# Sample scores of four batches side by side on TensorE, and the sample's rows spread over four partitions each, in a hybrid decoder step

## The chip, the core and the metric

The kernel runs on one core of a Trainium2 chip. The metric is the time of one execution on the device in microseconds; lower is better. TensorE multiplies matrices, VectorE and ScalarE work on tiles element by element, GpSimd does some of that and issues the gathers, SyncE issues the other DMAs. Each engine carries out its own instructions in order and waits for others by semaphores.

## The reference

One layer of a decoder is computed for a prompt of 512 rows and for a sample group of 8 batches with 4 new rows each (32 rows), width 1024. Cut to what matters here:

```python
mods = (silu(c) @ w_ada + b_ada)            # six rows of 1024 for the prompt and for each sample batch
h = rmsnorm(x, g_norm1) * (1 + mods[1]) + mods[0]
q, k, v, gates, z, xbc, dt = split(h @ w_in)
# sample attention, per batch of 4 rows: compressed blocks, 15 selected blocks of 64, a window of 512
s = q @ keys.T * SCALE ; p = masked_softmax(s) ; o = p @ values
att = g0 * o_cmp + g1 * o_sel + g2 * o_win   # 8 query heads on 2 key heads of 64
y_ssm = ssd_mixer(...)
mixed = concat([rmsnorm(att, g_att_out), y_ssm]) @ w_out
x = x + mods[2] * mixed
h = rmsnorm(x, g_norm2) * (1 + mods[4]) + mods[3]
y = x + mods[5] * hier_moe(h)                # top 1 of 4 groups, top 2 of 4 experts, 16 experts
```

Prompt and sample go through the same layer with the same weights; the sample reads its older keys and values from paged caches.

## The kernel before, in words

The program is one long function, `hybrid_step`. A framework schedules it: the code says what depends on what, and a list scheduler with its own estimate of durations lays every engine's instructions in a fixed order. `tc.high_priority(offset)` and `tc.add_manual_dep` (an order between two instructions) influence it; `in_turn` ties TensorE's instructions of some helpers to the order in which they are written. So a changed instruction can move others on every engine.

Four stages follow one another. First come the modulation rows and the input projection. The rows of modulation that are needed late are computed by `ada_block` (L290 on) into the tile `mods`, 128 partitions by 8 by 128: partition 32 j + r holds, for row r of nine (the prompt and eight batches), the j-th quarter of 512 columns. The tile is stored to DRAM as `modd` (L760) and read back from there as rows.

Second comes the attention. `attend(t, br)` computes the prompt's attention of row tile t (128 rows, eight heads): two products into PSUM (`s`), a maximum (L815), an exponential (L817), transpositions (L820) and value products (`ot`). Between them the sample's parts are laid. For half hb (four batches) and half h of a batch's past, `gather_half` (L1047) gathers 128 partitions x 8 rows per batch; `sel_part` works on them in two chunks `c4`. In a chunk, `transposed` (L1020 to L1026) turns one batch's keys, four 128x128 blocks into one PSUM bank of the tag `sm` (two buffers), and `evac` (L100 on VectorE, L102 on ScalarE) copies them to a tile `kt` (five buffers). Then one product per batch b4 writes that batch's scores to partitions 32 b4 to 32 b4 + 31 of the bank `smo`, behind a product with `Eb` that writes the mask. `win_half` does the same for the window without a mask. Two halves, two halves of the past, two chunks and two windows make ten groups of four scores. After the softmax the weights are turned and multiplied with the values (`weighted`).

Third come the out-projection and the router. The joined rows are turned and split into a high and a low part (`catH`, `catL`); the weight is split likewise (`wh` and `wl` for the first 512 columns, `wH` and `wL` for the last 512, L1692 and L1693). The sample's part of the product (`samp_k`) lies in PSUM with column quarter j on partitions 32 j to 32 j + 31, and `samp_out` copies the quarters side by side into 32 rows of 1024. Then the sample's residual (L1699, L1700), its normalised row `h2` (`sample_rows`, L1655 to L1668), the router's logits and `rank` follow in 32 partitions. `OSEQ` names the order in which prompt tiles (`m`, `f`, `r`) and the sample (`s`) are written. At the end the tokens are counted per expert and the first rows are gathered.

Fourth, 16 experts and one extra tile are worked off, three products each, with weights loaded ahead by SyncE. Weights of the first expert are issued between the constants of the out-projection.

The helper `mm` records every product under L92, and the copies of `evac` stand under L100 and L102.

## Time and profile before

| What | Value |
|---|---|
| median of 3 runs | 784.91 us (782.52 to 787.93) |
| the profiled execution | 787.62 us |
| its span, first to last instruction | 785.9 us |
| TensorE busy | 709.3 us (90%) |
| VectorE busy | 501.2 us (64%) |
| ScalarE busy | 355.2 us (45%) |
| GpSimd busy | 151.6 us (19%) |
| mean granted TensorE clock | 0.938 |
| DMA | 161.86 MB, mean 206 GB/s |

The profiled execution is one of its own; durations come from it. Busy time is the time in which an engine had at least one instruction under way. Matmuls overlap, so the time that one of them costs is read from its start to the start of the next. The granted clock is a share of TensorE's full speed.

### The profile page before, as it was taken

The page shows a single profiled execution, that of the slowest core. Times are in us where ns is not written, and L with a number is a line of the kernel's source. Part 1 is how long each engine was busy: PE and PEld are TensorE (multiplying, and loading weights), DVE is VectorE, ACT ScalarE, POOL GpSimd, SP SyncE. Part 2 cuts the span into 40 slices and gives each one's busy share as a digit, 9 for nine tenths or more (in the row PEclk, how much of TensorE's full clock was granted, in tenths as well). Part 3 has the DMA queues.
Part 4 walks back from the last instruction along what each step waited for, and adds up shares of the span by engine and source line. Part 5 has one row for each costly group of instructions (what it writes and reads, how often), then busy time and mean ns, then how long its engine had stood idle before and what let it go on. Part 6 is the DMA issues. An engine that isn't in the chain of part 4 may idle for free. (4 is left out here: it accounts for less than half of the span.)

```text
span 785.9 us, 14689 instructions
## 1 busy us (share of the span) xinstructions
PE 709.3 (90%) x5565; PEld 511.7 (65%) x5565; DVE 501.2 (64%) x1333; ACT 355.2 (45%) x813; POOL 151.6 (19%) x169
## 2 busy tenths in 40 slices
PE   4999999898999578998989999899668999999993
PEld 3667877676777355665647756687655766767562
DVE  5633692524644767554557555878986888877773
ACT  3423444515233333364434435613433766677661
POOL 1103012121321421010111200020131232233221
PEclk9999999889899879699999889999868999999997
DMA  8964895144559634423445041988767899997311
GB/s 286 355 187 131 289 330 193 58 162 161 214 191 346 253 143 172 149 81 134 164 158 219 2 108 23 360 267 286 290 253 282 270 333 335 334 329 256 86 25 23
DMA packets 67094, 161.86 MB, mean 206 GB/s; under 512 B 19005, under 2 KB 31238, under 8 KB 60622
## 3 DMA queue, kind: packets, MB, share of 16 engines
q1 hardware_dynamic: 56798, 115.54, 42.3%
q0 software_dynamic: 10224, 45.37, 17.5%
q8 instruction: 44, 0.72, 0.4%
q14 instruction: 28, 0.23, 0.1%
HBM read 153.48 MB, written 20.74 MB: 222 GB/s over the span
## 5 line engine op out<-in xcount | busy, mean ns | idle before, releaser
L92 PE MATMUL acc<-wh,hH 128*128 128x512 f32 (+1 forms) x128 | 48.9, 382 | 0.5 <-issue 0.5
L92 PE MATMUL acc<-wl,hH 128*128 128x512 f32 (+1 forms) x128 | 47.3, 370 | 0.0
L92 PE MATMUL acc<-wh,hL 128*128 128x512 f32 (+1 forms) x128 | 47.1, 368 | 0.0
L817 ACT ACTIVATE psb<-s,amx 128x128 f32<-128x128 f32 (+3 forms) x64 | 33.7, 528 | 27.4 <-DVE amx L815 24.3
L92 PE MATMUL acc<-gu,XF 128*128 128x512 f32 x88 | 46.1, 606 | 0.0
L92 PE MATMUL acc<-wh,XH 128*128 128x512 f32 x68 | 44.7, 657 | 0.4 <-ACT XH L1942 0.4
L815 DVE TENSOR_REDUCE amx<-s 128x1 f32<-128x128 f32 (+3 forms) x64 | 30.9, 484 | 17.3 <-PE s L92 17.3
L92 PE MATMUL ps<-wada,scT 128*32 128x128 f32 x768 | 38.0, 301 | 4.1 <-DMA wada<-in_w_ada 3.0
L92 PE MATMUL s<-KT,QT 128*128 128x384 f32 (+3 forms) x128 | 39.3, 392 | 1.3 <-DVE qa L838 0.8
L335 DVE TENSOR_TENSOR wl<-dn,wh 128x512 fp32r<-128x512 f32 x52 | 34.0, 686 | 7.0 <-ACT wh L334 6.9
L92 PEld LDWEIGHTS ps<-wada,scT 128*32 128x32 f32 x768 | 30.6, 122 | 10.3 <-issue 3.6
L1047 POOL DMA_INDIRECT gsel<-in_cache_sel,idx x16 | 20.6, 1289 | 84.3 <-PE smo L92 72.6
L334 ACT CAST wh<-dn 128x512 fp32r<-128x512 f32 x52 | 30.9, 619 | 12.9 <-PE acc L92 11.2
L820 PE MATMUL pt<-ident,psb 128*128 128x128 f32 x160 | 33.3, 308 | 3.3 <-ACT psb L817 3.3
L1991 POOL DMA_INDIRECT out_y_prompt<-yo,gi x13 | 21.4, 1646 | 74.8 <-DVE yo L1985 20.1
L335 DVE TENSOR_TENSOR wl<-gu,wh 128x512 fp32r<-128x512 f32 x44 | 29.5, 685 | 8.4 <-ACT wh L334 7.6
L92 PE MATMUL acc<-wh,HH 128*128 128x512 f32 x68 | 32.3, 478 | 1.6 <-ACT HH L1974 1.2
L334 ACT CAST wh<-gu 128x512 fp32r<-128x512 f32 x44 | 26.1, 619 | 15.8 <-PE acc L92 10.8
L92 PE MATMUL smo<-kt,Qb 128*32 128x512 f32 x80 | 29.6, 614 | 2.3 <-DVE kt L100 2.3
L102 ACT COPY kt<-sm 128x512 f32<-128x512 f32 x32 | 18.5, 584 | 27.6 <-PE sm L1023 24.0
L1985 DVE TENSOR_TENSOR yo<-acc,M 128x512 f32<-128x512 f32 x34 | 23.1, 686 | 11.5 <-PE acc L92 9.1
L92 PE MATMUL acc<-wl,HH 128*128 128x512 f32 x68 | 28.6, 421 | 0.0
(788 smaller groups left out, 1902.9 us busy)
## 6 DMA issues: line engine op xcount, KB each, us to landing
wada<-in_w_ada SPq DMA_DIRECT2D x24, 1024.0 KB
dn<-in_w_down SPq DMA_DIRECT2D x12, 1024.0 KB
gu<-in_w_gate SPq DMA_DIRECT2D x21, 512.0 KB
gu<-in_w_up SPq DMA_DIRECT2D x21, 512.0 KB
gux<-in_w_gate SPq DMA_DIRECT2D x11, 512.0 KB
gux<-in_w_up SPq DMA_DIRECT2D x11, 512.0 KB
wt<-in_cache_win SPq DMA_DIRECT2D x4, 1024.0 KB
wout<-in_w_out SPq DMA_DIRECT2D x4, 1024.0 KB
```

What stands on the lines that cost most here:

```text
L92: T.matmul(out, lhsT, rhs, start=start, stop=stop)
L102: S.copy(out, in_)
L334: S.copy(wh[:, 0:n], w)
L335: (eng or V).tensor_sub(wl[:, 0:n], w, wh[:, 0:n].bitcast(F32))
L815: V.tensor_reduce(mx, ps[:, 0:n], axis=AX.X, op=OP.max, negate=True)
L817: S.activation(pb[:, 0:n], ps[:, 0:n], AF.Exp, bias=mx, accum_out=sm[:, h:h + 1])
L820: T.transpose(pt[:, c * P:(c + 1) * P], pb[:, c * P:(c + 1) * P], ident)
L1047: G.indirect_dma_start(out=t.rearrange("p r c -> p (r c)"), out_offset=None, in_=sel_rows, in_offset=bass.IndirectOffsetOnAxis(ap=idx[:, 2 ...
L1985: V.tensor_tensor(yo[:, cols], po, M5[:, cols], op=OP.mult)
L1991: G.indirect_dma_start(out=y_p, out_offset=bass.IndirectOffsetOnAxis(ap=gi, axis=0), in_=yo, in_offset=None, bounds_check=511, oob_is_err= ...
```

## The change

The change has two parts. In the first, a helper `four_scores` issues the four products of a group one after the other, batch 3 first, with an order from each to the next; both `sel_part` and `win_half` call it. In the second, the sample's rows keep, from the out-projection to the router, the layout in which TensorE leaves them: row r's column quarter j of each half on partition 32 j + r, as 128 partitions by 2 by 128. The modulation rows for that are no longer read back from DRAM but picked from `mods` by a product with `pick` (one copy of each batch's row for its four sample rows), copied to `SMt` during the attention and to `SM4` afterwards; `mods` lives in a longer-lived pool for that. The sum of squares of a row is added over its four partitions by a product with `same4`. Loads and stores of such rows are four DMAs each.

```diff
-    mods = W(p1, [P, 8, P], F32, "mods", 1)
+    mods = smp.tile([P, 8, P], F32, name="mods", tag="mods")
...
-        if lhs is not None:
+        if lhs is not None and callable(dst):
             samp_out(ps, n, dst)
+        elif lhs is not None:
+            S.copy(dst, ps[:, 0:P])
...
+    def four_scores(hb, ps, kts, start=True):
+
+        last = None
+        for b4 in (3, 0, 1, 2):
+            b = 4 * hb + b4
+            i = T.matmul(ps[32 * b4:32 * b4 + 32, :], Qf[:, 32 * b:32 * b + 32], kts[b4], start=start, stop=True).ins
+            if last is not None:
+                tc.add_manual_dep(i, last.name, mybir.DependencyInfo(mybir.DependencyClass.NoSync,
+                                                                     mybir.DependencyReason.DATA), reason="four_scores")
+            last = i
...
-            for b4 in range(4):
-                b = 4 * hb + b4
-                mm(sc[32 * b4:32 * b4 + 32, :], Qf[:, 32 * b:32 * b + 32], kts[b4], start=False, stop=True)
+            four_scores(hb, sc, kts, False)
...
-        for b4 in range(4):
-            b = 4 * hb + b4
-            mm(sw[32 * b4:32 * b4 + 32, :], Qf[:, 32 * b:32 * b + 32], kts[b4])
+        four_scores(hb, sw, kts)
...
+    pick = W(p3, [P, 4, NB, TS], F32, "pick", 1)
+    V.tensor_copy(pick, ident.rearrange("p (j r) -> p j r", r=32)[:, :, 1:9, None].to_broadcast([P, 4, NB, TS]))
+    SMt = tl.tile([P, 6, P], F32, name="SMt")
+    for n0, n1 in ((0, 4), (4, 6)):
+        ps = PS("sm")
+        mm(ps[:, 0:P * (n1 - n0)], pick.rearrange("p j b t -> p (j b t)"), mods[:, n0:n1, :].rearrange("p n c -> p (n c)"))
+        S.copy(SMt[:, n0:n1, :].rearrange("p n c -> p (n c)"), ps[:, 0:P * (n1 - n0)])
     sel_second(1, gt11, *first1)
...
-    xs1 = W(p6, [NS, D], F32, "xs1", 1)
+    xs1 = W(p6, [P, 2, P], F32, "xs1", 1)
...
-    m0S, a2S, m3S = [W(p6s, [NS, D], F32, "MS", 3) for _ in range(3)]
-    mod_rowS(2, m0S)
-    mod_rowS(4, a2S)
-    mod_rowS(3, m3S)
+
+    SM4 = W(p6s, [P, 6, P], F32, "SM4", 1)
+    S.copy(SM4, SMt)
+    m0S, m3S, a2S = SM4[:, 0:2], SM4[:, 2:4], SM4[:, 4:6]
+    g24 = W(p6s, [P, 2, P], F32, "g24", 1)
+    for j in range(4):
+        SP.dma_start(g24[32 * j:32 * j + 32], dram(a["g_norm2"], j * P, [[0, NS], [512, 2], [1, P]]))
+    same4 = W(p6s, [P, 4, NS], F32, "same4", 1)
+    V.tensor_copy(same4, sel32[:, None, :].to_broadcast([P, 4, NS]))
...
-        SP.dma_start(h2d[512:512 + NS, :], h2)
+        for j in range(4):
+            SP.dma_start(h2d[512:512 + NS, :].rearrange("r (h j c) -> j r h c", h=2, j=4)[j], h2[32 * j:32 * j + 32])
...
-        V.tensor_tensor(lgS, router(h2, NS, wr, 0), rb[0:NS], op=OP.add)
-        V.tensor_tensor(lgS, router(h2, NS, wr, 1), lgS, op=OP.add)
+        with tc.high_priority(offset=100):
+            pt = PS()
+            for hf in range(2):
+                T.transpose(pt[:, hf * P:hf * P + P], h2[:, hf, :], ident)
+            hT = W(p6, [P, 2, 4, NS], F32, "h2T", 3)
+            evac(hT.rearrange("p h j r -> p (h j r)"), pt[:, 0:2 * P])
+            pr = PS("pr")
+            for k in range(KC):
+                mm(pr[0:NS, 0:20], hT[:, k // 4, k % 4, :], wr[:, k, :], start=k == 0, stop=k == KC - 1)
+            V.tensor_tensor(lgS, pr[0:NS, 0:20], rb[0:NS], op=OP.add)
         rank(4)
```

The same treatment stands in the places that are left out: `ss` and `h2` of `sample_rows` have 128 partitions, `mixS` is copied in two pieces of 128x128, `xs1` is loaded and `xsd` stored by four DMAs.

The order moves in three places. The first is TensorE in the attention, at the first selection group: `sm<-ident,gsel` are the four transpositions of one batch's keys, `smo<-Eb,mT` the mask, `smo<-kt,Qb` one batch's scores; `ot`, `s` and `pt` belong to the prompt. Before:

```order
L92 MATMUL smo_3324<-Eb_3013,mT_3291 128x512
L1023 MATMUL sm_3310<-ident,gsel_3186 128x128 x4
L92 MATMUL smo_3324<-kt_3301,Qb_2907 32x512
L92 MATMUL ot_3941<-ptsb_4042,selo 64x128
L1023 MATMUL sm_3317<-ident,gsel_3188 128x128 x4
L92 MATMUL smo_3324<-kt_3308,Qb_2907 32x512
L92 MATMUL smo_3324<-kt_3315,Qb_2907 32x512
L1023 MATMUL sm_3332<-ident,gsel_3182 128x128 x4
L836 MATMUL s_4051<-ident,psb_4046 128x128 x4
L92 MATMUL s_4413<-KT,QT 128x384 x2
L92 LDWEIGHTS identb
L92 MATMUL s_4413<-negm,identb 128x128
```

And after:

```order
L1025 MATMUL sm_3310<-ident,gsel_3186 128x128 x4
L92 MATMUL ot_3941<-ptsb_4042,selo 64x128
L1025 MATMUL sm_3317<-ident,gsel_3188 128x128 x4
L1025 MATMUL sm_3332<-ident,gsel_3182 128x128 x4
L838 MATMUL s_4051<-ident,psb_4046 128x128 x4
L92 MATMUL s_4413<-KT,QT 128x384 x2
L92 LDWEIGHTS identb
L92 MATMUL s_4413<-negm,identb 128x128
L1050 MATMUL smo_3324<-kt_3322,Qb_2907 32x512
L1050 MATMUL smo_3324<-kt_3301,Qb_2907 32x512
L1050 MATMUL smo_3324<-kt_3308,Qb_2907 32x512
L1050 MATMUL smo_3324<-kt_3315,Qb_2907 32x512
```

The four scores of the group, three pieces before (the last of them follows the rows shown), stand in a row behind the last key tile's transpositions and four rows of the prompt's.

The second place is the start of the out-projection, on ScalarE: `t,ssa` are the squares of the prompt's attention rows, `wh` and `wH` casts of the weight's two halves, `catH` the turned rows. Before:

```order
L1430 ACTIVATE t_1161_5438,ssa_5433<-qa 128x512
L1430 ACTIVATE t_1162_5440,ssa_5433<-qa 128x512
L1522 ACTIVATE catH_5515<-ps_5552,gcat 128x512
L1522 ACTIVATE catH_5515<-ps_5559,gcat 128x512
L334 CAST wh_5717<-wout_5702 128x512
L334 CAST wh_5733<-wout_5702 128x512
L1692 CAST wH<-wout_5706 128x512 x4
L1692 CAST wH<-wout_5708 128x512 x4
```

And after:

```order
L1447 ACTIVATE t_1162_5447,ssa_5442<-qa 128x512
L1447 ACTIVATE t_1163_5449,ssa_5442<-qa 128x512
L1517 COPY SM_1191_5543<-SMt 128x768
L334 CAST wh_5732<-wout_5717 128x512
L334 CAST wh_5748<-wout_5717 128x512
L1721 CAST wH<-wout_5721 128x512 x4
L1545 ACTIVATE catH_5524<-ps_5567,gcat 128x512
L1545 ACTIVATE catH_5524<-ps_5574,gcat 128x512
```

The copy to `SM4` is new, and six casts have moved ahead of the first `catH`. On TensorE, at the same place, the last prompt tile's transpositions (`s<-ident,psb`) end the attention before:

```order
L92 MATMUL smo_5360<-gsel_4814,kt_5389 32x128
L92 MATMUL smo_5360<-selnew_2883,snT_5356 32x128 x4
L836 MATMUL s_5261<-ident,psb_5256 128x128 x4
L1521 MATMUL ps_5552<-ident,zy 128x128 x4
L1521 MATMUL ps_5559<-ident,zy 128x128 x4
L92 MATMUL pr_5608<-osum_3029,RS_3004 32x64 x16
```

After, they stand ahead of the sample's value products, of which the first three are shown:

```order
L1025 MATMUL sm_5370<-ident,pbs_5278 128x128 x4
L1025 MATMUL sm_5393<-ident,pbs_5278 128x128 x4
L838 MATMUL s_5261<-ident,psb_5256 128x128 x4
L92 MATMUL smo_5369<-gsel_4808,kt_5375 32x128
L92 MATMUL smo_5369<-gsel_4810,kt_5375 32x128
L92 MATMUL smo_5369<-gsel_4812,kt_5375 32x128
```

So that row has moved ahead of all 32 value products and of `selnew`.

The third place is VectorE at the end of the router: rows with 32 partitions are the sample's logits and its ranking (`rkb`, `rk`, `og`, `Ab`), `t<-acc` is the last prompt tile's result (in both pieces that of the last mixed tile). Before, where `t<-acc` stands seven rows ahead of the first row shown:

```order
L1710 COPY lg<-pr_6078 128x20
L1645 TENSOR_TENSOR rkb_6050<-lg 32x20x4
L1646 TENSOR_TENSOR rkb_6050<-lg 32x20x4
L1648 TENSOR_TENSOR rkb_6050<-rkb_6050,msk_5697 32x160
L1731 TENSOR_SCALAR ms_1340_6363<-ss_1338_6360,ms_5885 128x1
L1740 TENSOR_TENSOR h_1318_6260<-x_5501,M 128x512
L1650 TENSOR_REDUCE rk<-rkb_6050 32x20
L122 TENSOR_SCALAR rsq_yh_1341_6365<-ms_1340_6363 128x1
L1733 TENSOR_TENSOR lg<-pr_6136,lg 128x20
L1651 TENSOR_SCALAR og<-rk 32x4
L1734 SCALAR_TENSOR_TENSOR lg<-lg,rsq_zh_1291_6121,rbP_5687 128x20
L1652 SCALAR_TENSOR_TENSOR Ab<-rk,og 32x16
```

And after:

```order
L1669 TENSOR_TENSOR rkb_6056<-lg 32x20x4
L1773 SCALAR_TENSOR_TENSOR h_1300_6178<-h_1300_6178,rsq_zh_1307_6215,M 128x512 x2
L1671 TENSOR_TENSOR rkb_6056<-rkb_6056,msk_5712 32x160
L1740 COPY lg<-pr_6084 128x20
L100 COPY h2T_6170<-ps_6165 128x512
L1673 TENSOR_REDUCE rk<-rkb_6056 32x20
L1674 TENSOR_SCALAR og<-rk 32x4
L1675 SCALAR_TENSOR_TENSOR Ab<-rk,og 32x16
L1770 TENSOR_TENSOR h_1317_6266<-x_5510,M 128x512
L1753 TENSOR_TENSOR t_1325_6312<-acc_6287,M 128x512
```

The sample's ranking now stands ahead of the last mixed tile's result, not behind it.

## Rows read from the trace of the kernel before

**Rows 1.** Windows by stage: length, busy us of each engine (instructions), clock, DMA share, GB/s.

```profile
288.00:490.00 202.00, 192.58 (x1544) 123.93 (x1542) 116.26 (x337) 89.08 (x246) 24.23 (x34) 0.93 0.33 116
490.00:552.00 62.00, 59.96 (x435) 47.48 (x433) 49.70 (x124) 24.17 (x57) 6.92 (x6) 1.00 0.88 303
552.00:577.00 25.00, 12.57 (x143) 11.84 (x142) 23.45 (x93) 11.34 (x19) 6.97 (x8) 0.72 0.60 231
```

**Rows 2.** TensorE's timeline in the attention: start, us, engine, line, tiles, count, [idle before].

```profile
290.96 1.04 PE L92 MATMUL smo<-kt,Qb 128*32 128x512 f32 x2
291.94 0.33 PE L820 MATMUL pt<-ident,psb 128*128 128x128 f32 x1
...
338.30 1.07 PE L92 MATMUL smo<-kt,Qb 128*32 128x512 f32 x8
339.30 0.43 PE L92 MATMUL ot<-ptsb,wino 128*64 128x128 f32 x2
...
402.93 1.04 PE L92 MATMUL smo<-kt,Qb 128*32 128x512 f32 x2 [2.30 <-DVE kt L100]
...
475.72 1.04 PE L92 MATMUL smo<-kt,Qb 128*32 128x512 f32 x2
```

**Rows 3.** Groups of instructions, 288 to 500 us: busy us, mean ns, idle before, releaser.

```profile
L92 PE MATMUL smo<-kt,Qb 128*32 128x512 f32 x80 | 29.6, 614 | 2.3 <-DVE kt L100 2.3
L102 ACT COPY kt<-sm 128x512 f32<-128x512 f32 x31 | 17.9, 584 | 27.6 <-PE sm L1023 24.0 <-PE sm L1277 3.4
L100 DVE COPY kt<-sm 128x512 f32<-128x512 f32 x22 | 15.1, 688 | 15.3 <-PE sm L1023 14.2 <-PE sm L1277 1.0
```

**Rows 4.** TensorE's timeline at a 512-column float32 product of the sample's state.

```profile
448.55 1.12 PE L92 MATMUL sm<-pbs,s2k 32*128 32x512 f32 x2
449.60 0.88 PE L92 MATMUL ot<-ptsb,selo 128*64 128x128 f32 x12
```

**Rows 5.** ScalarE's timeline from the out-projection's start to the first expert's weights.

```profile
492.09 1.25 ACT L1522 ACTIVATE catH<-ps,gcat 128x512 fp32r<-128x512 f32 x2
493.23 1.14 ACT L334 CAST wh<-wout 128x512 fp32r<-128x512 f32 x2
494.26 4.27 ACT L1692 CAST wH<-wout 128x512 fp32r<-128x512 f32 x8
...
567.95 2.18 ACT L334 CAST wh<-gu 128x512 fp32r<-128x512 f32 x4 [3.75 <-issue]
```

**Rows 6.** TensorE's timeline around the end of the attention.

```profile
485.12 1.73 PE L92 MATMUL smo<-gsel,kt 128*32 128x128 f32 x54
...
488.70 0.66 PE L836 MATMUL s<-ident,psb 128*128 128x128 f32 x4
...
493.90 1.19 PE L92 MATMUL acc<-wh,catH 128*128 128x512 f32 x4 [1.76 <-ACT wh L334]
```

**Rows 7.** Groups of instructions on VectorE, 490 to 552 us.

```profile
L1700 DVE TENSOR_TENSOR xs<-xs,h2S 32x1024 f32<-32x1024 f32 x1 | 2.2, 2194 | 0.0
...
L1699 DVE TENSOR_TENSOR h2S<-h2S,MS 32x1024 f32<-32x1024 f32 x1 | 1.2, 1205 | 0.0
...
L1538 DVE TENSOR_TENSOR catS<-pr,gcat 128x256 f32<-128x256 f32 x1 | 0.4, 417 | 0.0
```

**Rows 8.** SyncE's timeline, the store of the sample's residual.

```profile
532.80 0.32 SPq L1701 DMA_DIRECT2D xsd<-xs  x1
```

**Rows 9.** VectorE's timeline in the routing: the sample's ranking, the prompt's last.

```profile
554.21 0.22 DVE L1645 TENSOR_TENSOR rkb<-lg 32x80 f32<-32x80 f32 x1
...
556.87 0.15 DVE L1652 SCALAR_TENSOR_TENSOR Ab<-rk,og 32x16 bf16<-32x16 f32 x1
...
568.70 0.17 DVE L1652 SCALAR_TENSOR_TENSOR Ab<-rk,og 128x16 bf16<-128x16 f32 x1
```

**Rows 10.** Windows at two places of the attention (columns as in rows 1).

```profile
315.00:330.00 15.00, 14.22 (x65) 9.82 (x64) 9.66 (x28) 5.62 (x22) 1.45 (x2) 0.57 0.52 184
...
400.00:405.00 5.00, 2.70 (x18) 1.63 (x17) 2.98 (x7) 1.52 (x3) 0.72 (x1) 1.00 0.90 360
```

More of the change, by code (lines that the diff above doesn't have):

```diff
@@ L959, in hybrid_step @@
     V.tensor_copy(X4, ident[0:64, 0:64, None].to_broadcast([64, 64, 4]))
-    sel32 = C3([P, 32], F32, "sel32")
+    sel32 = const([P, 32], F32, "sel32")
     V.tensor_reduce(sel32, ident.rearrange("p (j r) -> p r j", r=32), axis=AX.X, op=OP.add)
@@ L1509, in hybrid_step @@
     V.tensor_scalar_mul(M[:, 2, :], M[:, 2, :], -1.0 / 8192)
-    V.scalar_tensor_tensor(a2S, a2S, 1.0, g2[0:NS], op0=OP.add, op1=OP.mult)
+    V.scalar_tensor_tensor(a2S, a2S, 1.0, g24, op0=OP.add, op1=OP.mult)
     V.tensor_scalar_mul(a2S, a2S, -1.0 / 8192)
     SP.dma_start(x1, a["x_prompt"].rearrange("o (t p) d -> p (o t) d", p=P))
-    SP.dma_start(xs1, a["x_sample"].rearrange("b t d -> (b t) d"))
+    for j in range(4):
+        SP.dma_start(xs1[32 * j:32 * j + 32], dram(a["x_sample"], j * P, [[D, NS], [512, 2], [1, P]]))
     ko = (4, 5, 6, 7, 0, 1, 2, 3)
@@ L1655, in sample_rows @@
     def sample_rows():
-        h2 = W(p6s, [NS, D], F32, "h2S", 1)
-        ss = W(p6, [NS, 1], F32, "ss2")
+        h2 = W(p6s, [P, 2, P], F32, "h2S4", 1)
+        ss = W(p6, [P, 1], F32, "ss2")
         S.activation(h2, xs1, AF.Square, accum_out=ss)
-        x = W(p6, [NS, 1], F32, "ms2")
-        V.tensor_scalar(x, ss, 1.0 / D, EPS, op0=OP.mult, op1=OP.add)
+        ps = PS("pr")
+        mm(ps[:, 0:1], same4.rearrange("p j r -> p (j r)"), ss)
+        x = W(p6, [P, 1], F32, "ms2")
+        V.tensor_scalar(x, ps[:, 0:1], 1.0 / D, EPS, op0=OP.mult, op1=OP.add)
         r = rsqrt_col(x, "h2s")
@@ L1663, in sample_rows @@
         V.tensor_add(h2, h2, m3S)
-        SP.dma_start(h2d[512:512 + NS, :], h2)
+        for j in range(4):
+            SP.dma_start(h2d[512:512 + NS, :].rearrange("r (h j c) -> j r h c", h=2, j=4)[j], h2[32 * j:32 * j + 32])
         lgS = lg[0:NS, 4, :]
-        V.tensor_tensor(lgS, router(h2, NS, wr, 0), rb[0:NS], op=OP.add)
-        V.tensor_tensor(lgS, router(h2, NS, wr, 1), lgS, op=OP.add)
+        with tc.high_priority(offset=100):
[8 more added lines that the diff above has]
+            V.tensor_tensor(lgS, pr[0:NS, 0:20], rb[0:NS], op=OP.add)
         rank(4)
-    mixS = W(p6s, [NS, D], F32, "h2S", 1)
+    mixS = W(p6s, [P, 2, P], F32, "mixS", 1)
     w0 = load_w(w_out, 0, 512, "wout", (1, 0))
     w1 = load_w(w_out, 512, 512, "wout", (1, 0))
-    def to_mix(n):
-        def f(src, c0, c1):
-            S.copy(mixS[:, 512 * n + c0:512 * n + c1], src)
-        return f
     wL = [SLOT([P, 4, 512], F32R, "wL") for _ in range(2)]
-    acc = proj(p6u, catH, catL, catS, w0, 512, to_mix(0), ks=ko)
+    acc = proj(p6u, catH, catL, catS, w0, 512, mixS[:, 0], ks=ko)
     close_p6u()
@@ L1697, in hybrid_step @@
     early("u")
-    samp_out(ps, 512, to_mix(1))
+    S.copy(mixS[:, 1], ps[:, 0:P])
     V.tensor_mul(mixS, mixS, m0S)
     V.tensor_add(xs1, xs1, mixS)
-    SP.dma_start(xsd, xs1)
+    for j in range(4):
+        SP.dma_start(xsd.rearrange("r (h j c) -> j r h c", h=2, j=4)[j], xs1[32 * j:32 * j + 32])
     h2s = {}
```

## The prediction

> **What bounds the kernel now.** I read the stages first: the busy time of each engine in the stretches that the change touches [rows 1]. From 288 to 490 us lies the attention, where the sample batches' scores are computed; TensorE is busy in 192.58 of 202.00 us, VectorE in 116.26, ScalarE in 89.08. From 490 to 552 us lies the out-projection, again TensorE's (59.96 of 62.00). From 552 to 577 us the routing of the tokens is finished, and there it is VectorE that is busy in 23.45 of 25.00 us while TensorE stands half the time. From 577 us on the experts run, and the change doesn't touch them. So what the change takes from TensorE counts before 552 us, what it takes from VectorE only in the short stretch behind it, and what it takes from VectorE between 490 and 552 us counts for nothing by itself.
>
> Then I read TensorE's timeline for the scores [rows 2]. One score is two matmuls of 128x512 onto 32 of the 128 output partitions. A row of the timeline merges neighbours of one kind: the scores stand in 27 such rows, the first at 290.96, the last at 475.72. One batch alone (x2) starts at 290.96 and the next instruction at 291.94: 0.98 us. Where the scheduler happened to put four batches side by side (x8), they start at 338.30 and the next instruction at 339.30: 1.00 us for all four. Four batches in a row therefore cost what one costs alone. Of the ten groups of four (eight selections, two windows) only that one stands whole today; the others are split into two to four pieces.
>
> **The scores in a row (first part of the change).** After it the order on TensorE has ten pieces in place of 27: 17 x 0.98 = 16.7 us less, and I take 16.5, since a piece of four was 0.02 longer. Two of the 27 ran at a lower clock and were dearer; I don't count on that. TensorE's share of the stretch, 192.58 / 202.00 = 0.953, is the part that shows as time: -15.7 us.
>
> Against that stands a new wait. The first score of a group (batch 3, chosen because its keys come last) waits for the last of four transposed key tiles, and everything behind it on TensorE, the prompt's attention too, waits with it. Such a copy takes 584 ns on ScalarE or 688 ns on VectorE [rows 3]. Today the same matmuls stood 2.3 us in all for their keys, in one place, 402.93 [rows 2, 3]. The bounds are 0, if other work always lies between, and 10 x 2.30 = 23 us, if every group stands like that one. In the new order seven of the ten groups have at least a microsecond of prompt matmuls between the last transposition and the first score, and an eighth has two wide matmuls there; the two others have two short rows. I take +1.5 us, near the lower bound because the gap is filled in eight of ten. Key tiles are also held longer, four of the five buffers at once; the fifth lets one transposition of the next group run ahead, and that is inside the same bounds.
>
> **Modulation rows by a matmul (second part).** The sample's rows of modulation now come from the tile `mods` by a product with a picking matrix: 512 and 256 columns in float32, 128 output rows. The nearest row is a 512-column float32 product, at 448.55, whose successor starts at 449.60: 1.05 us [rows 4]. So 1.05 + 0.53 = 1.6 us of TensorE, bounded by 0 (it fills a gap) and 3.2 (it falls into a slow-clock stretch); times 0.953, +1.5 us. The two copies out of PSUM (584 ns [rows 3] and less) lie on ScalarE, which is busy 44% of the stretch; the picking matrix is one small copy on VectorE, busy 58%. Nothing for those.
>
> **Out-projection's start.** On ScalarE the order changes: behind the last squares now come a copy of 128x768, two casts `wh` and four casts `wH`, and only then the first `catH`, which TensorE's first product needs. Today `catH` starts at 492.09, and that product starts at 493.90, 1.81 us later, having stood 1.76 us [rows 5, 6]. After: the copy between 0.58 and 1.17 (once and twice the 128x512 one [rows 3]), I take 0.8; two `wh` 1.14, half of the eight `wH` 2.13, one `catH` 0.63: 4.7 us, so 2.9 us later. But the order on TensorE moves too: the last prompt tile's transpositions (today at 488.70) now stand before the sample's value products instead of behind them. Today those begin at 485.12 [rows 6]; of the 3.58 us between, 1.0 was other work, so ScalarE's chain starts 2.6 us earlier against TensorE. Net +0.3 us, with bounds -0.7 (the copies and casts hidden) and +2.9 (the lead lost).
>
> **Four partitions to a row.** Between 490 and 552 us the sample's 32x1024 operations become 128x256. Today they take about 1.2 us each, one of them 2.19; a 128x256 one takes 0.42 [rows 7]. There are six such steps on VectorE and one on ScalarE, some 5 us less on VectorE, but under TensorE's 59.96 of 62.00 us: 0. New on TensorE is a one-column product that waits for the sum of squares; it stands behind the first 27 products of the remaining half, and the shorter steps ahead of it should be done by then: 0, at most about 1 us if the sum is late. On SyncE's queue six issues of 128 KB go and sixteen of 32 KB come, ten more in all; an issue such as the one at 532.80 takes 0.32 us [rows 8], so 3.2 us of queue. Three half-megabyte loads of the first expert's weights are moved behind the loads of the out-projection's constants. Their first reader is at 567.95 [rows 5], over 40 us later: 0. If that cover went, one half-megabyte load would show.
>
> **The routing stretch.** The sample's ranking stands today in VectorE's full stretch, from 554.21 to 556.87 + 0.15, and the last ranking of the prompt ends there at 568.70 [rows 9]. In the new order it stands ahead of the last mixed tile, while TensorE still multiplies. From its first to its last row are 2.8 us, in which other work lies too; that is the most that can go. Nothing is gained (0) if the last tile's own chain, not VectorE's backlog, sets 568.70. VectorE stands only 1.55 of the 25 us [rows 1], so I go nearer to the upper end: -2.0.
>
> **The sum.** -15.7 + 1.5 + 1.5 + 0.3 - 2.0 = -14.4 us. Against the profiled execution (787.62 us, of which 785.9 are the span) that is 773.2. This execution lies 2.7 us above the median of the runs, 784.91; the same -14.4 on the median gives **770.5 us**.
>
> **A rule that speaks against it.** A key tile costs a copy of 584 or 688 ns, and ten groups need four each [rows 3], while TensorE now needs 1.00 us for four scores. The Trainium skill ("TensorEngine Tiling (Array Packing)", Performance Considerations) says that packing matmuls speeds up TensorE but not the emptying of PSUM, which may then become the bottleneck. This is the first rival below; by the rows VectorE and ScalarE are far from full in this stretch, so I give it a fifth.
>
> **Rivals.**
> *Evacuation takes TensorE's place.* Each group stands for a whole copy and the hand-over on both sides, about 1 us, ten times. For it: the copies of `kt` waited for TensorE, so they follow it closely, and every group now needs all four. Against it: [rows 1], and the filled gaps in the new order. Price: +10 in place of +1.5, sum -5.9, **779 us**.
> *The scores don't run side by side.* Four in a row would cost 4 x 0.98; then the first term is nil: +1.5 + 1.5 + 0.3 - 2.0 = +1.3, **786 us**. The eight matmuls at 338.30 speak against it.
> *The clock falls: slower.* TensorE's granted clock is 0.93 over the attention [rows 1], a mixture of its two levels, 2.4 and 1.2 GHz: from 315 to 330 us it is 0.57, though TensorE is busy in 14.22 of 15 us there [rows 10]. If less work on TensorE lets the clock fall more often, its remaining 176 us of work grow by 176 x (0.93 / c - 1). The gain is eaten at c = 0.86; from c = 0.825 the kernel is slower by over 1%; at 0.80 it is 787.62 + 28.6 - 14.4, **799 us** on the median's scale. Against it: from 400 to 405 us TensorE was busy in 2.70 of 5 us and kept 1.00 [rows 10]. The Trainium skill ("TensorE: Matmul & The Clock Gate", Part 1) says that the slow state is the default and that activity releases it; the second of these rows doesn't show such a fall.
> *A slow stretch disappears.* If the new order leaves out the one at 315 us, whose loss is 15 x 0.43 = 6.4 us, or half of it, the sum is -18 to -21, **765 us**.
>
> **Chances.** The forecast 0.65 (its own range 766 to 776: the waits at 0 to 6, the routing at 0 to -2.8), evacuation 0.20, no packing 0.03, clock falls 0.04, a slow stretch gone 0.08. The range reaches down to the fourth rival and up past the first: 764 to 781. One per cent, 7.8 us, is about what a measurement of this kernel can tell from no change: below 777.1 lie the forecast, the last rival and a third of the first, 0.79; above 792.8 the clock's and a little for what I have not seen, 0.05; between, 0.16.
>
> **What would show it.** Right: the score rows on TensorE's timeline all read x8 with about 1.07 us; the attention ends some 11 to 14 us earlier than at 490; the routing stretch is about 2 us shorter; the out-projection's first product stands no more than 2 to 3 us. Wrong: rows of x8 preceded by idle time that ends with `kt` (evacuation); rows of x8 that last 2 us or more at full clock (no packing); a granted clock below 0.88 in the attention (clock); or a stand of 4 us and more where ScalarE casts `wH` ahead of `catH`.

## The result and the profile after

The changed kernel ran at 780.23 us (median of 20 runs, 773.51 to 785.28), the kernel before, beside it, at 786.84 us (20 runs, 780.33 to 793.7). The ratio is 0.9928, with an interval of 0.9902 to 0.9954: some 5.7 us less, where 14.4 had been forecast. The time lies in the range that was given (764 to 781), but the step is less than half as large, and within the 1 per cent that I had called no change. Ratios, clocks and the lines through them leave out runs more than 1.5 per cent above the fastest of their kernel (one of the changed kernel's 20 here, two of the six of part one with wide products below), the medians of time don't.

The profiled execution of the changed kernel took 784.75 us, its span is 783.0. It is one of the slower ones: its mean granted clock is 0.918, the median of the runs 0.926. First TensorE's scores in the attention, on its timeline; there are ten such rows in place of 27 [rows 2], the first at 296.08, the last at 473.03, all with eight matmuls. One of them stands for its keys. Two more stands follow that the trace of before doesn't have in this form: the transposition of the softmax's `sn` behind one group, and the first product of the out-projection.

```profile
381.35 1.07 PE L1050 MATMUL smo<-kt,Qb 128*32 128x512 f32 x8
385.46 0.40 PE L1017 MATMUL sm<-ident,sn 128*32 128x128 f32 x1 [3.04 <-ACT sn L1015]
...
400.73 1.06 PE L1050 MATMUL smo<-kt,Qb 128*32 128x512 f32 x8 [0.46 <-ACT kt L102]
...
455.04 2.93 PE L92 MATMUL sm<-mods,pick 128*128 128x512 f32 x4
...
489.40 0.50 PE L92 MATMUL acc<-wh,catH 128*128 128x512 f32 x1 [2.17 <-ACT catH L1545]
```

The group of the scores (busy us, mean ns of one, idle before) shows the saving itself; it answers to the first row of [rows 3]:

```profile
L1050 PE MATMUL smo<-kt,Qb x80: 592/605/617, 296.1 to 473.5; 128*32 128x512 f32 x80
L1050 PE MATMUL smo<-kt,Qb 128*32 128x512 f32 x80 | 10.7, 605 | 0.5 <-ACT kt L102 0.5
```

TensorE is busy with scores for 10.7 us in place of 29.6, and the 80 matmuls stood 0.5 us for keys in place of 2.3. So the scores do run side by side, and the keys come in time.

The same stretches as in [rows 1] (length, busy us of each engine with instructions, granted clock, DMA share, GB/s):

```profile
288.00:490.00 202.00, 185.40 (x1591) 127.21 (x1591) 123.68 (x359) 97.32 (x264) 26.17 (x38) 0.90 0.35 124
490.00:552.00 62.00, 61.18 (x434) 50.81 (x432) 44.57 (x117) 18.40 (x40) 4.61 (x3) 0.97 0.90 303
552.00:577.00 25.00, 15.09 (x119) 14.03 (x119) 22.41 (x91) 10.42 (x18) 5.84 (x8) 0.50 0.46 166
```

The clock is lower in all three: 0.90 against 0.93, 0.97 against 1.00, 0.50 against 0.72. (The windows stand at fixed times and the changed kernel is some 3 to 4 us ahead, so the last pair is in part a shift; from the first product of the out-projection to the last ranking it is 0.89 against 0.96.) Where, windows over single places show. First the changed kernel, then the kernel before at its own places and, in the last row, at the same stretch of the out-projection's end:

```profile
428.00:443.00 15.00, 15.00 (x88) 10.17 (x85) 8.56 (x21) 3.25 (x9) 5.96 (x15) 0.54 0.01 1
445.00:460.00 15.00, 15.00 (x38) 6.35 (x38) 6.77 (x32) 2.75 (x6) 0.37 (x1) 0.54 0.23 61
551.00:562.00 11.00, 10.24 (x50) 10.27 (x50) 9.83 (x46) 4.23 (x7) 2.21 (x2) 0.53 0.71 278
```

```profile
433.00:440.00 7.00, 7.00 (x34) 5.58 (x33) 3.15 (x8) 2.81 (x8) 4.04 (x4) 0.51 0.02 4
453.00:461.00 8.00, 8.00 (x33) 5.08 (x32) 3.70 (x15) 1.17 (x2) 0.00 (x0) 0.57 0.42 88
551.00:562.00 11.00, 10.43 (x103) 10.09 (x99) 9.94 (x46) 5.73 (x10) 1.88 (x1) 1.00 0.98 394
```

Both kernels run the sample's state part and its neighbours between 428 and 461 us. Before, 15 us of that are near the lower level (1.2 GHz); after, 30 us, with TensorE busy in every one of them. And the last 11 us of the router's products, at full clock before (103 matmuls), are at 0.53 after (50 matmuls in as many microseconds). The same group of eight takes nearly twice as long, first before, then after:

```profile
557.00 0.97 PE L92 MATMUL pr<-wrP,h2T 128*128 128x20 f32 x8
...
554.35 1.73 PE L92 MATMUL pr<-wrP,h2T 128*128 128x20 f32 x8
```

If I multiply, microsecond by microsecond, TensorE's busy time by what the clock lacks to 1.00, the span of before loses 34.9 us to the clock and that of the changed kernel 50.8. That is 15.9 more, while the span is 2.9 shorter. By stretches, with the second profile of the changed kernel (from the experiments) beside it, in us of TensorE's work:

| Stretch, us | Before | Changed | Changed again |
|---|---|---|---|
| 0 to 288, ahead of the scores | 13.0 | 17.1 | 17.8 |
| 288 to 490 | 14.5 | 20.4 | 16.9 |
| 490 to 585 | 4.1 | 10.3 | 8.7 |
| from 585 | 3.2 | 3.1 | 4.9 |
| all | 34.9 | 50.8 | 48.3 |

So the larger part of what is lost in addition lies outside the attention.

Along the way the lead grows and shrinks. The same exponential of the prompt's attention (the 44th of 64) starts at 419.90 before and 403.98 after: 15.9 us ahead. The 57th starts at 461.91 and 460.69: 1.2 ahead. That isn't the clock alone, since the new order lays more of the other work between the two: 369 matmuls in place of 286. Part one alone, in the experiments, tells the two apart. The first product of the out-projection is 4.5 us earlier (493.90 to 489.40), the last ranking 2.9 (568.70 to 565.81), and so is the end (785.9 to 783.0).

One profile could be chance, since slow stretches come and go from run to run. So the first question for the runs was whether the clock or the new stands took the gain.

### The profile page after: what moved, and what is told of

It reads as the page before. It is cut to its first block, busy times and chain, and to the rows that moved or that the text cites. A ratio compares the mean times of both kernels' runs of the same rounds, so it can differ in the third digit from the quotient of the medians.

```text
span 783.0 us, 14706 instructions
## 1 busy us (share of the span) xinstructions
PE 705.2 (90%) x5565; PEld 519.5 (66%) x5565; DVE 500.0 (64%) x1334; ACT 355.6 (45%) x809; POOL 145.6 (19%) x169
## 5 line engine op out<-in xcount | busy, mean ns | idle before, releaser
L334 ACT CAST wh<-dn 128x512 fp32r<-128x512 f32 x52 | 30.9, 620 | 10.7 <-PE acc L92 10.1
L1060 POOL DMA_INDIRECT gsel<-in_cache_sel,idx x16 | 16.9, 1058 | 82.0 <-PE smo L92 68.7
L822 PEld LDWEIGHTS pt<-ident,psb 128*128 128x128 f32 x160 | 18.9, 149 | 16.0 <-ACT psb L819 7.6
L92 PE MATMUL acc<-wl,XH 128*128 128x512 f32 x68 | 28.8, 423 | 0.6 <-DVE wl L335 0.6
```

What stands on the lines that cost most here:

```text
L92: T.matmul(out, lhsT, rhs, start=start, stop=stop)
L334: S.copy(wh[:, 0:n], w)
L822: T.transpose(pt[:, c * P:(c + 1) * P], pb[:, c * P:(c + 1) * P], ident)
L1060: G.indirect_dma_start(out=t.rearrange("p r c -> p (r c)"), out_offset=None, in_=sel_rows, in_offset=bass.IndirectOffsetOnAxis(ap=idx[:, 2 ...
```

## The experiments

Each run of a kernel lists its mean granted clock, and so do the runs of before beside it. The table has them all, in the order of the four jobs, each on another chip. "At equal clock" is a reading of mine: within a job I put a straight line through time against clock of the runs of before, and take how far the kernel's mean lies from that line at its own mean clock. The line's slope was 5.2, 6.1, 5.8 and 6.9 us for each 0.01 of clock in the four jobs. It is a correlation, and the mean clock also counts time in which TensorE stands. For the kernels at 0.92 to 0.93 the line is also carried to the edge of what the runs of before cover (0.928 to 0.953) or past it; the changed kernel's own runs, 20 and 12, give 6.4 and 5.7 us for each 0.01. So I read it to a few microseconds.

| Kernel | Median us | Ratio (interval) | Median clock, before's beside it | At equal clock |
|---|---|---|---|---|
| part one alone | 776.49 | 0.9881 (0.9833 to 0.9929) | 0.9345, 0.9425 | -12.6 |
| part two alone | 792.04 | 1.0065 (1.0031 to 1.0100) | 0.928, 0.9425 | +0.4 |
| the change again | 780.01 | 0.9947 (0.9914 to 0.9981) | 0.9255, 0.9425 | -13.1 |
| the change, 17 wide products | 774.12 | 0.9850 (0.9802 to 0.9898) | 0.9355, 0.9425 | -13.9 |
| the change, `catH` first | 781.29 | 0.9983 (0.9950 to 1.0016) | 0.921, 0.941 | -13.5 |
| the change, rows by DMA | 777.40 | 0.9916 (0.9880 to 0.9951) | 0.9345, 0.941 | -10.8 |
| the change, router with wide products | 778.81 | 0.9966 (0.9931 to 1.0002) | 0.9265, 0.941 | -12.1 |
| part one, 15 wide products | 770.62 | 0.9830 (0.9765 to 0.9895) | 0.9445, 0.941 | -13.2 |
| the change, wide products first | 810.47 | 1.0312 (1.0253 to 1.0370) | 0.918, 0.941 | +12.3 |
| the change, 17 narrow products | 775.23 | 0.9887 (0.9832 to 0.9941) | 0.9305, 0.941 | -16.3 |
| part two, rows by DMA | 786.11 | 1.0012 (0.9973 to 1.0050) | 0.936, 0.938 | 0.0 |
| the change, rows by DMA, 15 wide products | 771.92 | 0.9823 (0.9778 to 0.9868) | 0.9385, 0.938 | -13.2 |

### The two parts, and the change again

Part one alone is the kernel before with `four_scores` and its two calls. Part two alone is the changed kernel with the two calls undone:

```diff
-            four_scores(hb, sc, kts, False)
+            for b4 in range(4):
+                b = 4 * hb + b4
+                mm(sc[32 * b4:32 * b4 + 32, :], Qf[:, 32 * b:32 * b + 32], kts[b4], start=False, stop=True)
...
```

> The kernel before with the four scores in a row alone; the sample's rows keep their old layout. First theory (clock): the scores save what was forecast, about 14 us, and the slower TensorE clock between 428 and 460 us, which the trace of the changed kernel shows, takes most of it back. If that slow stretch comes with the earlier arrival at the sample's state products, it is here too, mean clock about 0.926, time 778 to 782 us. If it comes from the picking products of the second part, the clock stays at 0.938 and the time is 772 to 774 us. Rival (waits): the clock is chance, and the new waits of the second part (ScalarE's casts ahead of the first turned rows, the picking products) ate the gain; then this kernel runs at 771 to 774 us with any clock.

> The changed kernel with its scores written as before, one batch at a time: the second part alone. The forecast's terms for that part sum to -0.2 us (picking products +1.5, start of the out-projection +0.3, routing -2.0): 786.6 us, the same as before. If the second part costs time (waits, or a clock that falls at the end of the out-projection), 789 to 793 us. If its gain was underrated, below 784 us.

> The changed kernel once more, for a second profile and for the granted clock of each run. First theory (clock): the half-clock stretches at 428 to 442, 445 to 460 and 551 to 579 us stand in this profile too, the mean clock of the runs is 0.92 to 0.93, and runs with a higher clock are the faster ones by about 8 us for each 0.01. Rival (chance): the stretches stand elsewhere or are gone, at the same median of about 780 us.

By the ratios and the 785.51 us of before in this job, part one gains 1.19 per cent, 9.3 us, and part two loses 0.65 per cent, 5.1 us. The two add up to what the whole change gives here, 0.53 per cent, 4.2 us; each of the three has an interval of 3 to 4 us to either side. Part one came out between the two times that I had given it, and so did its clock. Both have a lower clock than before, by 0.008 and 0.0145, and the whole change by 0.017. In its second profile the stretch from 428 to 441 us is at 1.00, the one from 441 to 456 again at 0.54:

```profile
428.00:441.00 13.00, 11.92 (x112) 8.32 (x108) 9.97 (x24) 3.99 (x12) 5.97 (x15) 1.00 0.01 1
441.00:456.00 15.00, 15.00 (x43) 6.87 (x41) 6.92 (x31) 2.92 (x7) 0.95 (x1) 0.54 0.26 69
```

So neither theory holds as I put it. A given slow stretch isn't fixed: of the two before 460 us, one is gone here. But the lower mean clock is there in all three sets of runs. The rival (the clock is chance, the waits of part two ate the gain) would have had part one at 771 to 774 us. Its stands are small. In the profile of part one the attention is over at 475.78, and the stretches behind it take as long as before (74.91 against 74.80 us from the first product to the last ranking):

```profile
288.00:475.78 187.78, 172.73 (x1566) 120.27 (x1566) 118.27 (x343) 90.91 (x250) 25.61 (x38) 0.95 0.38 133
475.78:550.69 74.91, 69.70 (x503) 57.20 (x504) 63.46 (x186) 29.74 (x63) 8.44 (x4) 0.95 0.84 297
```

Between the 44th and the 57th exponential of the prompt part one does about the work of the whole change, 370 matmuls against 369 (of which four are the picking products). First part one alone, then the whole change:

```profile
398.57:448.14 49.57, 47.21 (x370) 32.81 (x368) 32.63 (x96) 18.51 (x52) 9.93 (x19) 0.86 0.26 92
403.98:460.69 56.71, 54.35 (x369) 35.45 (x367) 33.08 (x98) 18.77 (x53) 10.31 (x19) 0.76 0.27 95
```

Before takes 42.01 us there, for 286 matmuls at 0.84. So of the 14.7 us of lead that the changed kernel loses here about half is work that has moved into the stretch (part one loses 7.6 at a clock no lower than before's), and the other 7.1 come at a lower clock, with the picking products among them.

### What of part two costs

The rows of modulation go through DRAM, and the picking products, the copies to `SMt` and to `SM4` and the long-lived `mods` are gone:

```diff
-    mods = smp.tile([P, 8, P], F32, name="mods", tag="mods")
+    mods = W(p1, [P, 8, P], F32, "mods", 1)
...
+        SP.dma_start(msd[j], mods[32 * j + 1:32 * j + 9, 0:6, :].rearrange("r n c -> r (n c)"))
...
-    S.copy(SM4, SMt)
+    for j in range(4):
+        SP.dma_start(SM4[32 * j:32 * j + 32].rearrange("p n c -> p (n c)"),
+                     dram(msd.rearrange("j b c -> j (b c)"), j * NB * 6 * P, [[6 * P, NB], [0, TS], [1, 6 * P]]))
```

> The changed kernel without the picking products: the sample's rows of modulation go through DRAM (four stores in the first stage, four loads at the out-projection), mods lies in its old pool again, and the copy to SM4 is gone too. If the picking products (1.6 us at full clock, 2.9 at half) and the copy ahead of the out-projection cost what the second part loses, 776 to 778 us. If the second part loses at the router (small products ahead of the last wide ones, the clock falls 13 to 15 us ahead of the last ranking in place of 7 to 9), nothing changes: 779 to 781 us.

> The second part alone (scores one batch at a time), with the rows of modulation through DRAM in place of the picking products, and mods in its old pool: no picking products, no two copies, no copy to SM4. The second part alone ran at 1.0065 of before, with the clock at 0.928 against 0.940. If the picking products and what belongs to them cost that, this runs at 0.998 to 1.001 and a clock near 0.938. If the router's order costs it, at 1.004 to 1.008 and a clock near 0.93.

With the whole change this gave 0.9916 against 0.9947 and 0.9928, too close to tell. With part two alone it is 1.0012 in place of 1.0065, and the clock that of before (0.936 beside 0.938, in place of 0.928 beside 0.9425). The two ran in different jobs, and their intervals overlap by 0.002. So most of what part two loses very likely belongs to the picking products and what goes with them. The router's order isn't cleared by that: with the rows by DMA, too, its stretch is longer than before in the profile (76.32 us, below). The products themselves are 2.93 us in the profile, at half clock. Which of the pieces (products, two copies, the small copy that makes `pick`, the pool of `mods`) lowers the clock isn't separated.

One place at which it falls can be named, and it lies 190 us ahead of the products. The order moves in a fourth place, that I had not listed: where the prompt's queries and keys are turned (`qhl`, `khl`), ahead of the attention. Before, VectorE starts the first copy of turned queries (`QT`) at 259.58; after, it starts at 261.39, behind a run of small steps of which the new `pick` is one, and TensorE stands longer for the second group. Before, then after:

```profile
260.33 0.66 PE L913 MATMUL s<-ident,qhl 128*128 128x128 f32 x4 [0.78 <-DVE QT L100]
...
260.89 0.66 PE L915 MATMUL s<-ident,qhl 128*128 128x128 f32 x4 [2.27 <-ACT QT L102]
...
261.19 0.21 DVE L1436 COPY pick<-ident 128x128 f32<-128x128 f32 x1
```

From the first of these products to the first score of the prompt, in before, the changed kernel, part two alone and part two with the rows by DMA:

```profile
258.45:276.87 18.42, 11.22 (x68) 8.09 (x64) 17.04 (x59) 7.75 (x18) 8.77 (x18) 0.81 0.81 300
257.53:277.54 20.01, 14.36 (x68) 11.15 (x64) 16.59 (x54) 7.87 (x18) 8.84 (x18) 0.60 0.81 290
256.81:276.75 19.94, 13.86 (x68) 10.22 (x64) 16.59 (x54) 8.11 (x19) 9.38 (x19) 0.66 0.80 292
258.37:276.49 18.12, 11.12 (x68) 8.07 (x64) 16.74 (x58) 7.76 (x18) 8.18 (x18) 0.81 0.80 293
```

All six profiles of kernels without the picking products have 18.1 to 19.3 us here, at clocks of 0.74 to 0.82. Of the eight with them seven have 19.9 to 20.5 us, at 0.50 to 0.66; the eighth (the router with wide products) has 17.02 at 0.90. So some 1.6 us of part two's loss stands here, long before a picking product runs. What moved this order (`pick`, the pool of `mods`, or the scheduler's weighing of all that follows) was not tried.

Two other suspects of part two were tried. The first fell; the try at the second brought a cost of its own and decides nothing about it. In the first, ScalarE's casts of `wH` come behind the first two `catH`:

```diff
-        S.copy(wH[:, k, :], w1(k))
+        i = S.copy(wH[:, k, :], w1(k)).ins
+        tc.add_manual_dep(i, cat[1].name, mybir.DependencyInfo(mybir.DependencyClass.NoSync,
+                                                               mybir.DependencyReason.DATA), reason="cat_first")
```

> The changed kernel with an order on ScalarE: the casts of wH come behind the second turned row block (catH). In both profiles of the changed kernel TensorE stands 2.17 us for that block and then runs four microseconds at half clock, which costs 1.7 us more. If this start of the out-projection is where the second part loses, the block is there about 2 us earlier and the clock holds: 776 to 778 us against 780. Rival: the casts were needed soon after anyway, the stand moves to them, and nothing changes (779 to 781 us).

The first product now follows the `osum` product at once (482.39, without a stand), and the stretch is at full clock. But from there to the turning of the sample's rows (`pr<-ident,atS`) it takes 24.4 us in place of 21.2, and the time is no better, 0.9983 against 0.9947 and 0.9928. The casts were needed; the rival holds.

In the second, all 96 wide products of the out-projection's second half get a priority over the small ones:

```diff
         for k in ko:
-            mm(acc, catH[:, k, sl], wH[:, k, :], start=k == ko[0], stop=False)
...
+        with tc.high_priority(offset=100):
+            for k in ko:
+                mm(acc, catH[:, k, sl], wH[:, k, :], start=k == ko[0], stop=False)
...
```

> The changed kernel with its 96 wide products of the out-projection's second half ahead of all small ones (the sample's and the prompt's router), by a priority on them. In the changed kernel the last 10 wide ones stand behind the sample's router, and the clock falls 13 to 15 us ahead of the last ranking; before, all stood ahead of it, and it fell 7 us ahead. If that order is what the second part costs, the work lost to the clock in the routing falls from 7 to 1 to 4 us and the time to 776 to 778 us. Rival: the sample's chain is late now (its sum of squares waits for the last wide product) and the time is 781 us or more.

It is 3 per cent slower, 23 us. The sample's chain is late, as the rival said, and far more than I had thought: TensorE stands 7.74 us for it at the end, with the prompt's router queued behind, and the last ranking comes 107.2 us behind the first product in place of 76.4.

```profile
564.28 0.66 PE L1695 MATMUL ps<-ident,h2S 128*128 128x128 f32 x2 [7.74 <-DVE rsq_zh L124]
```

### Can the clock be given back?

Two kernels add products without use to the sample's state part of the changed kernel, one ahead of each group of small products, into the PSUM tile that the group then overwrites. There are 17 (not 16 as I had written). In one they are 512 columns wide, in the other 8:

```diff
+    def warm(ps, n=1):
+        for _ in range(n):
+            mm(ps, Eb[:, 0:16, :].rearrange("p j e -> p (j e)"),
+               Eb[:, 0:16, :].rearrange("p j e -> p (j e)")[:, None, :].to_broadcast([P, 4, P]))
...
     pe = PS("sm")
+    warm(pe, 1)
```

> The changed kernel with 16 added products without use, 128x512 in bf16, one ahead of each group of small products of the sample's state (their results are overwritten). Each costs about 0.2 us at full clock, 3.4 us in all. First theory (clock): wider products in that stretch keep the clock up there; the two slow stretches from 428 to 460 us cost 13.6 us of TensorE's work in the profile, so the time falls by up to 10 us, to 770 to 777 us. Rival (the clock there is not the cause, or the wider products don't hold it): slower by the added work, 783 to 785 us.

> The changed kernel with the 17 added products of the run that gained 6 us, at the same places, but 8 columns wide in place of 512: under 0.1 us each. If the wide ones worked by holding the clock, these gain nothing: both slow stretches between 428 and 460 us (or one of them) stand, 779 to 782 us. If they worked by the order that the added instructions make, or by filling TensorE's gaps, these work as well: 772 to 775 us.

Windows over the state part: the changed kernel's own two profiles have 0.67 and 0.84 from 418 to 460 us. With the wide products the clock is full there:

```profile
418.00:450.00 32.00, 31.25 (x231) 20.56 (x231) 22.86 (x63) 11.06 (x30) 7.23 (x16) 1.00 0.18 70
```

And with the narrow ones nearly so:

```profile
418.00:450.00 32.00, 30.65 (x239) 21.71 (x239) 23.16 (x60) 11.54 (x31) 5.80 (x6) 0.95 0.22 79
```

Against the change run again the wide products gain 0.010 of before, with intervals that don't meet. The narrow ones gain 0.006 in another job, with intervals that overlap; that they gain is likely, but not clear of noise. The wide ones' six runs have clocks of 0.933 to 0.941, the narrow ones' 0.920 to 0.933, the changed kernel's 0.920 to 0.932. So the theory that width alone holds the clock is in doubt: the narrow ones, which do next to no work, seem to bring a gain of time too. Both kernels also move a few of the prompt's products to other places between the small ones, since the scheduler lays the order anew. Whether the products, their width or that order raises the clock stays open; for that, one order would have to be forced on all three kernels, which wasn't tried. What the wide products do show is that TensorE can be given more work and the kernel be faster.

The same on part one alone, and on the whole change with the rows by DMA, with 15 products (none ahead of the picking products, which aren't there):

> Part one alone with 15 added wide products in the sample's state part (as in the earlier run with the whole change, without the two ahead of the picking products). If the two effects add, 776.5 - 6 = 770.5 us, 769 to 773. In the profile of part one alone the half-clock stretch from 423 to 437 us loses 6.8 us; it should be gone, for 3 us of added work. Rival: the clock's gain belongs to the changed kernel's own stretches (two, 13.6 us), and here the added work eats it: 775 to 778 us.

> The whole change with the rows of modulation through DRAM and the 15 added wide products in the sample's state part. If the gains of the two add (0.003 and 0.008 to 0.010 of before), the ratio is 0.981 to 0.985, as good as part one with the added products (0.983). If both act on the same loss, 0.985 to 0.992.

Both are as forecast, 0.983 and 0.982, the lowest ratios of all (though not clear of the 0.985 with 17 wide products) and faster than both kernels of this case. In the first the attention is over at 470.54, at a clock of 0.96:

```profile
288.00:470.54 182.54, 168.69 (x1563) 116.70 (x1561) 116.56 (x339) 89.00 (x245) 26.01 (x38) 0.96 0.39 136
```

The last kernel tried the same in the router: one wide product ahead of each group of transpositions for the prompt's logits.

```diff
             pt = PS()
+            if n == P:
+                mm(pt, onesb, onesb[:, None, :].to_broadcast([P, 4, P]))
```

> The changed kernel with eight added products without use, 128x512 in bf16, one ahead of each group of transpositions for the prompt's router (overwritten by them); 8 x 0.2 = 1.6 us at full clock. If the clock that falls at the end of the out-projection is what the second part costs, it stays up longer there: the work lost to it in the routing, 6.5 to 7.6 us in the two profiles, falls to 1 to 4 us and the time to 777 to 779 us. Rival: VectorE sets the pace there and the clock costs nothing; 780 to 782 us.

The clock stayed low there all the same, 0.52, and 0.9966 can't be told from the change alone:

```profile
546.00:558.00 12.00, 9.71 (x59) 8.78 (x58) 11.02 (x49) 6.41 (x9) 1.26 (x1) 0.52 0.45 179
```

## Why the prediction was half right

**The scores (-15.7): right.** 27 pieces became ten, and the piece of four costs what one cost. Part one alone lies 12.6 us under the line of before at equal clock, where I had forecast 14.2 with the waits (+1.5). That is the reading of a line, to a few microseconds.

**The waits for the last key (+1.5): right in size, but at another place.** The keys cost 0.5 us, 1.8 less than before. What stands instead is the chain behind a group: for a window's scores, maximum, exponential and transposition follow with nothing of the prompt's left to lay between, 3.04 us at 385.46 in the changed kernel, and the same in part one alone:

```profile
380.27 0.40 PE L1015 MATMUL sm<-ident,sn 128*32 128x128 f32 x1 [3.12 <-ACT sn L1013]
```

That is +1.2 in all. But behind the stand the clock is at 0.57 from 384 to 392 us, which is another 2.9 us of work, and I had not counted that a wait can be followed by slow work. The first rival, evacuation, is out: it wanted 10 us of waiting for keys. The Trainium skill ("TensorEngine Tiling (Array Packing)", Performance Considerations) names the emptying of PSUM as what may bound packed matmuls; no row here shows that.

**The picking products (+1.5): under-sized.** They and what goes with them cost 0.53 per cent, some 4 us (1.0065 with, 1.0012 without, each to 3 us to either side). 2.93 us is their place in the profile; the clock is lower with them in both pairs of kernels (0.9255 against 0.9345, 0.928 against 0.936). And "the picking matrix is one small copy on VectorE, busy 58%. Nothing for those" was a term put at nothing by VectorE's mean share of the attention. That copy lies in a stretch ahead of it, where TensorE waits for VectorE's copies; with it and the pool of `mods` this stretch takes 20.01 us in place of 18.42.

**The out-projection's start (+0.3): as good as right.** The first product stands 2.17 us for `catH`, as the last section had it (2 to 3), in place of 1.76. What I had left out is that in the two profiles of the changed kernel the clock falls for 4 us right behind this stand, 1.7 us of work. But taking the stand away brought nothing. The order on ScalarE is the one that I had read from the order of instructions:

```profile
484.83 0.81 ACT L1517 COPY SM<-SMt 128x768 f32<-128x768 f32 x1
485.55 1.13 ACT L334 CAST wh<-wout 128x512 fp32r<-128x512 f32 x2
486.59 2.17 ACT L1721 CAST wH<-wout 128x512 fp32r<-128x512 f32 x4
488.67 1.25 ACT L1545 ACTIVATE catH<-ps,gcat 128x512 fp32r<-128x512 f32 x2
```

**The routing (-2.0): nothing.** From the first product to the last ranking it takes 76.4 and 75.3 us in the two profiles of the changed kernel, 74.8 before. The sample's ranking did move ahead of the last tile's (the first row below, beside [rows 9]; the second is the prompt's last):

```profile
547.44 0.16 DVE L1675 SCALAR_TENSOR_TENSOR Ab<-rk,og 32x16 bf16<-32x16 f32 x1
...
565.81 0.17 DVE L1675 SCALAR_TENSOR_TENSOR Ab<-rk,og 128x16 bf16<-128x16 f32 x1
```

But TensorE's router products, at full clock before, run at 0.53. I had read VectorE's 23.45 of 25.00 us as the bound and not asked at which clock TensorE's part of that chain would run. With part two alone and the rows by DMA it is 76.32 us as well (487.20 to 563.52). That the slow products eat what the ranking gained is my reading of the profiles; the run that was to raise the clock there didn't raise it. One profile speaks for it: in the changed kernel with 17 wide products the clock fell later in this stretch, and the stretch is 1.5 us shorter than before:

```profile
481.41:554.75 73.34, 69.74 (x499) 59.12 (x500) 57.63 (x177) 26.79 (x54) 5.87 (x4) 0.93 0.86 303
```

The nine other profiles with part two have 75.3 to 79.1 us at 0.89 to 0.93 here (leaving out the kernel with its wide products first), those without it 74.8 to 74.9 at 0.95 to 0.96.

**The clock: the step that failed.** I set the sum at the clock of before ("Two of the 27 ran at a lower clock and were dearer; I don't count on that"), and gave the rival "the clock falls" 0.04. It was priced by 176 x (0.93 / c - 1) for the attention alone. With the 0.90 that the profile has, that is +5.9 us: -14.4 + 5.9 = -8.5. In the second profile of the changed kernel the same stretch has 0.92, which is +1.9. But pricing the attention alone left out the larger part: of the 15.9 and 13.4 us of work that the two profiles lose in addition, some 10 and 11 lie ahead of 288 and behind 490 us. The clock over all runs is 0.017 lower than before, which at 5.2 us for each 0.01 is +8.8. So of the forecast 14.4, 13.1 are there at equal clock, and about nine of them are given back by the clock: 4.2 remain in that job, 5.7 in the first comparison. Where 15 added products bring the clock to that of before (0.9445 beside 0.941, 0.9385 beside 0.938), the gain is 0.0170 and 0.0177 of before, 13 to 14 us, near the 14.4. The clock of the attention stayed above the 0.88 that I had named as the sign of this rival. My error was the question, and the stretch: I had asked only whether the clock falls in the attention so far that the kernel gets slower, and not what a fall of two hundredths over the whole kernel takes from the gain. Why it falls more often in the changed order stays open. The last rival (the slow stretch at 315 us disappears) came about in the first profile of the changed kernel, whose clock from 315 to 330 us is 1.00, and not in the second (0.66); other slow stretches made up for it.

**Why I thought it wouldn't fall.** One stretch of before in which TensorE was half idle (400 to 405 us) kept the full clock, and I took that for evidence. The rows at 445 to 460 us show the other side: busy in 15.00 of 15 us, and at 0.54. Neither row lets one forecast the clock from the busy share. The Trainium skill ("TensorE: Matmul & The Clock Gate", Part 1) has the slow state as that of an engine that has been idle and has activity release it; in that row the busy time of the trace and the clock don't go together in this way.

## What to carry to other kernels

Before a saving on TensorE is counted at the present clock, see how much of the span lies at half clock now, and price a few hundredths up and down as a term of the sum, not as a rare rival: here 0.01 was worth 5 to 7 us of 785. Compare kernels by time and clock together; at equal clock every variant with part one reads -11 to -16 (but for the one that made the sample's chain late), and both with part two alone 0. A small copy counts by what waits behind it at its place, not by its engine's mean share. And where four products go in a row, look for what stood between them: the next chain, here the softmax, may need that filling more than the products needed company.

## What was unexpected in the hardware

The runs of one and the same kernel differ by the clock. The kernel before took 778.20 us at a mean clock of 0.953 and 789.08 at 0.934, in one job on one chip; through its 20 runs the correlation of time and clock is -0.97. TensorE had a mean granted clock of 0.54 over 15 us in which it was busy throughout (445 to 460 us). Added products, 17 of 512 columns, made the kernel 6 us faster (774.12 against 780.01); 17 of 8 columns gave 0.9887 of before, on another chip, between the changed kernel's 0.9947 and the 0.985 of the wide ones.
